# A Hymba-style decoder layer: six depthwise filters as three half-length ones, gate dots off VectorE, and a planner that knows the shared port

## The chip, the cores and the metric

The kernel runs on one core of one Trainium2 chip, in one launch. The metric is the device time of an execution in microseconds (us), the median of several runs. A profile of one execution is read beside it. Engines are named as in the profile: PE is TensorE (PEld its weight loads), DVE is VectorE, ACT is ScalarE, POOL is GpSimd, SP is SyncE, which issues the DMAs.

## The reference

x is 1024 tokens of 1024 channels in float32; there is one layer.

```python
mod = silu(c) @ mod_w + mod_b                       # shift, scale, gate: 1024 each
h = rmsnorm(x, norm_g) * (1 + scale) + shift
u = h @ w_in                                        # 5 x 1024 columns: cv, cg, cs, lx, ls
v = cv * sigmoid(cg)
v = causal_depthwise_conv(v, dw_w, dw_b)            # 31 taps along the tokens, per channel
v = silu(layernorm(v, cln_g, cln_b))
y_conv = (v @ pw2_w + pw2_b) * silu(cs)
xs = causal_depthwise_conv(lx, sc_w, sc_b)          # 4 taps
r, i = sigmoid(xs @ wr + br), sigmoid(xs @ wi + bi) # 8 heads of 128
a = exp(-8 * r * softplus(-lam))
h_t = a_t * h_{t-1} + sqrt(1 - a_t^2) * (i_t * xs_t)
y_lru = h * silu(ls)
x = x + (1 + gate) * (concat(y_conv, y_lru) @ w_out)
out = rmsnorm(x, final_g)
```

## The kernel before

Channels lie on the 128 partitions and the 1024 tokens along a row, so a tile is 128 x 1024 and each 1024-wide tensor is eight tiles. Each matmul is done as three, on numbers split into a high part and a rest: high by high, high weight by rest, rest of the weight by high (`uh`, `ul`, `yh`, `yl` for data, `whi`, `wlo` for weights; `xsh`, `xsl` for the input of the gates). ACT makes a high part, DVE or POOL the rest. A weight tile takes 48 matmuls of 512 columns.

The stages: four weight tiles (`FIRST`, the conv value and gate of channels 0 and 1) run on x before its norm is known, and are scaled by `rbc` (the norm's factor, spread over the partitions by small matmuls from sums of squares, `sq`) and shifted by `bias` afterwards. Then 36 weight tiles of `w_in` follow, numbered 4 to 39, and with them, for each of eight heads i, two gate matmuls (`gate`, L928) behind the tile that makes `xs` of that head, whose four-tap filter runs on DVE. Weight tiles 40 to 47 are the second half of `w_out`, on the recurrent half's result. In between come the conv tiles: six of eight are filtered on DVE (`conv_tile`, 30 SCALAR_TENSOR_TENSOR in place on `cacc`, the only accumulator in PSUM of its pool, after a first pass on ACT), tiles 2 and 5 (`POOLED`) by products on ACT and sums on POOL. `csum` adds the eight; the mean of the layer norm is a matmul on it. The last stage does the pointwise projection and the first half of `w_out` as products on quarters of the matrices, with fewer multiplications.

The conditioning's 24 rows of 1024 are dot products on DVE (`modw`): eight for scale and eight for shift at the start, eight for `gate1` later (`gate_mod`), which the last additions need.

No order is written out by hand. `Plan` gathers operations with an engine, an estimated cost, a priority (mostly the number of the weight tile; conv tiles have 1000 + 5 i, so they fill gaps), the tiles they read and write, and goes through time, giving each engine the ready operation of lowest priority. What comes out is a fixed order for each engine's queue; on the chip an engine waits at the head of its queue and does nothing behind it. One rule of the planner is for GpSimd and VectorE, whose operations on two SBUF operands it lets run only one at a time:

```python
if o.lock:
    end = max(t, locked) + cost
    locked = end
```

The constants that the change touches: `GM` is the number of the weight tile with the first gate dot, `SQP` the priority of the squares of x.

Of the kernel before, what the change touches and what calls it, by code (L numbers as in the profile page):

```python
# [66 lines left out]
class Buf:  # L67
    def __init__(self, pool, name, dtype, parts):
        self.pool, self.name, self.dtype, self.parts = pool, name, dtype, parts
        self.left, self.tile = 0, None  # L70

# [4 lines left out]
class Op:  # L76
    __slots__ = ("eng", "cost", "emit", "prio", "table", "bufs", "succ", "wait", "ready",
                 "seq", "reserve", "columns", "lock", "end")


class Plan:
# [23 lines left out]
    def op(self, eng, cost, emit, prio, r=(), w=(), table=None, after=(), reserve=0,  # L105
# [25 lines left out]
        for b in o.bufs:  # L131
            b.left += 1
        self.ops.append(o)
        return o

    def order(self):
# [9 lines left out]
        locked = 0.0  # L146
        left = len(self.ops)
        while left:
            while releases and releases[0][0] <= t:
                free[heapq.heappop(releases)[2]] += 1  # L150
            moved = False
            for e in engines:
                if until[e] > t + 1e-9:
                    continue
                best, key = None, None
                for o in pending[e]:
# [9 lines left out]
                    if any(free[p] < n for p, n in need.items()):  # L166
                        continue
# [15 lines left out]
                if o.lock:  # L183
                    end = max(t, locked) + cost
                    locked = end
                o.end = end
                until[e] = end
                out.append((t, o))
                for b in o.bufs:
# [3 lines left out]
                    b.left -= 1  # L193
                    if b.left == 0 and b.pool in free:
                        heapq.heappush(releases, (end, b.name, b.pool))
                for s in o.succ:
                    lat = 0.0 if e == "PE" and s.eng == "PE" else 0.11 if e == s.eng == "DVE" else self.LATENCY[e]
                    s.ready = max(s.ready, end + lat)
                    s.wait -= 1
                    if s.wait == 0:  # L200
                        pending[s.eng].append(s)
            if not moved:
                nxt = [u for u in until.values() if u > t + 1e-9]
# [17 lines left out]
def hymba_layer(ctx: ExitStack, tc: tile.TileContext, xT, c_row, vecs, mod_w, w_first, w_in,  # L221
# [205 lines left out]
    def acc_tile(name, parts=2):  # L427
        return S.buf("acc", name, F32, parts)
# [405 lines left out]

    v, c = {}, {}
    csum = big_buf("csum")

    def conv_tile(i):
# [388 lines left out]
```

## Time and profile before

| what | us |
|---|---|
| median of three runs (769.9 to 771.56) | 771.23 |
| the profiled execution | 771.67 |
| its span, first to last instruction | 769.1 |
| PE busy | 733.7 (95%) |
| PEld busy | 605.0 (79%) |
| DVE busy | 699.6 (91%) |
| ACT busy | 400.6 (52%) |
| POOL busy | 313.4 (41%) |

The mean granted TensorE clock is 0.985 of full speed. "Busy" adds up the time in which an engine has an instruction running. A wait row names the engine that waited, and whose work ended the wait. A group row names the source line (of a helper in most cases), engine and operation, output and inputs, shapes and count, then busy time, mean of one in ns, and idle time before them with who ended it. A timeline row has start, duration, engine, line and operation, and in brackets the idle time just before it.

### The profile page before, as it was taken

To read this page: it belongs to the slowest core of one execution; us is meant where nothing else is said; L and a number is where in the kernel's file an instruction comes from. 1 tells how busy PE (TensorE), PEld (TensorE's weight loads), DVE (VectorE), ACT (ScalarE), POOL (GpSimd) and SP (SyncE) were. 2 spreads that over 40 slices of the span, in tenths; PEclk is the share of its full clock that TensorE was granted. 3 is DMA by queue.
4 is the path that set the end of the run, shared out by engine and by line. 5 is a ranking of instruction groups with operands and counts; after the bars stand their busy time and mean duration, and the time that the engine had idled before them with its cause. 6 is when DMAs were issued, how large, how long until landed. Compare 5 with 4: busy or idle time off the path is not lost.

```text
span 769.1 us, 8497 instructions
## 1 busy us (share of the span) xinstructions
PE 733.7 (95%) x3288; PEld 605.0 (79%) x3288; DVE 699.6 (91%) x720; ACT 400.6 (52%) x432; POOL 313.4 (41%) x124
## 2 busy tenths in 40 slices
PE   3998999999999999999997999999999999999995
PEld 2887778888888788888885888887888888887885
DVE  7989999999999999999999979999699976998565
ACT  6720737987516479755525575514575223544220
POOL 0040123999996769999981226122120000000000
PEclk9999999999999999999998999999999999999997
DMA  9940221323321112112110012334333432325114
GB/s 339 392 153 1 84 82 35 110 82 110 117 82 56 35 55 83 34 55 83 50 60 28 28 55 82 137 137 143 131 110 110 164 110 71 121 83 178 41 55 165
DMA packets 24951, 77.81 MB, mean 101 GB/s; under 512 B 2768, under 2 KB 6096, under 8 KB 24912
## 3 DMA queue, kind: packets, MB, share of 16 engines
q1 hardware_dynamic: 24912, 77.28, 28.3%
q8 instruction: 26, 0.43, 0.2%
q14 instruction: 13, 0.11, 0.0%
HBM read 64.68 MB, written 12.58 MB: 100 GB/s over the span
## 4 chain that ended last, share of the span: by engine, by line
PE 66%; DVE 14%; POOL 14%; issue 2%; DMA 2%; ACT 1%; DVEq 0%; POOLq 0%; SPq 0%; ACTq 0%
PE ps L410 43%; POOL c L292 9%; PE papw L531 5%; PE pbpw L531 4%; POOL wlo L292 3%; PE paout L531 3%; PE out L577 3%; DVE ul L284 2%; DVE cacc L284 2%; PE gate L928 2%; PE pbout L531 2%; PE first L639 2%; DVE modw L284 2%; DMA fraw<-in_w_first_dram 1%; DVE xs L284 1%
## 5 line engine op out<-in xcount | busy, mean ns | idle before, releaser
L292 POOL TENSOR_TENSOR wlo<-raw,whi 128x1024 fp32r<-128x1024 f32 x44 | 122.7, 2788 | 235.1 <-ACT whi L265 235.1
L410 PE MATMUL ps<-uh,wlo 128*128 128x512 f32 x576 | 178.3, 391 | 3.3 <-POOL wlo L292 3.2
L410 PE MATMUL ps<-ul,whi 128*128 128x512 f32 x576 | 178.0, 390 | 1.4 <-DVE ul L284 1.4
L410 PE MATMUL ps<-uh,whi 128*128 128x512 f32 x576 | 178.0, 390 | 0.0
L292 POOL TENSOR_TENSOR c<-c,cq 128x1023 f32<-128x1023 f32 (+29 forms) x60 | 160.0, 2667 | 7.7 <-ACT cq L273 5.0
L284 DVE SCALAR_TENSOR_TENSOR cacc<-sig,V,cacc 128x994 f32<-128x994 f32 (+28 forms) x116 | 147.2, 1269 | 3.4 <-ACT cacc L273 0.6
L410 PEld LDWEIGHTS ps<-uh,wlo 128*128 128x128 f32 x576 | 108.1, 188 | 27.2 <-POOL wlo L292 5.0
L410 PEld LDWEIGHTS ps<-ul,whi 128*128 128x128 f32 x576 | 108.4, 188 | 24.4 <-DVE ul L284 1.8
L410 PEld LDWEIGHTS ps<-uh,whi 128*128 128x128 f32 x576 | 108.3, 188 | 22.7
L265 ACT CAST whi<-raw 128x1024 fp32r<-128x1024 f32 x48 | 50.2, 1046 | 53.9 <-issue 26.6
L284 DVE SCALAR_TENSOR_TENSOR cacc<-first_u,V,cacc 128x994 f32<-128x994 f32 (+28 forms) x58 | 73.5, 1268 | 1.2
L273 ACT ACTIVATE cq<-sig,V 128x1023 f32<-128x1023 f32 (+29 forms) x60 | 63.7, 1127 | 2.3 <-POOL c L292 2.3
L273 ACT ACT_TABLE_LOAD x46 | 59.0, 1283 | 1.5 <-PEq L1219 0.7
L284 DVE SCALAR_TENSOR_TENSOR modw<-modw,sc 128x1024 f32<-128x1024 f32 x24 | 41.5, 1740 | 1.6 <-DMA modw<-in_mod_w_dram 1.6
L265 ACT CAST xsh<-xs 128x1024 fp32r<-128x1024 f32 x8 | 8.4, 1048 | 61.9 <-DVE xs L284 61.9
L410 PE MATMUL ps<-yh,whi 128*128 128x512 f32 x128 | 40.0, 394 | 0.0
L410 PE MATMUL ps<-yl,whi 128*128 128x512 f32 x128 | 39.5, 390 | 0.0
L410 PE MATMUL ps<-yh,wlo 128*128 128x512 f32 x128 | 39.4, 389 | 0.0
L639 PE MATMUL first<-uh,fhi 128*128 128x512 f32 x64 | 26.8, 418 | 12.5 <-ACT uh L273 11.0
L284 DVE SCALAR_TENSOR_TENSOR xs<-ps,V,xs 128x1023 f32<-128x1023 f32 (+2 forms) x24 | 30.6, 1275 | 3.4 <-ACT xs L273 3.4
L410 PEld LDWEIGHTS ps<-yh,whi 128*128 128x128 f32 x128 | 23.9, 188 | 5.2 <-issue 0.5
L410 PEld LDWEIGHTS ps<-yh,wlo 128*128 128x128 f32 x128 | 24.0, 188 | 5.1
(292 smaller groups left out, 1331.0 us busy)
## 6 DMA issues: line engine op xcount, KB each, us to landing
raw<-in_w_in_dram SPq DMA_DIRECT2D x36, 512.0 KB, 3.4
modw<-in_mod_w_dram SPq DMA_DIRECT2D x24, 512.0 KB, 5.4
raw<-in_w_out_dram SPq DMA_DIRECT2D x12, 512.0 KB, 4.2
scsd<-scs SPq DMA_DIRECT2D x8, 512.0 KB, 3.0
acc<-in_xT_dram SPq DMA_DIRECT2D x8, 512.0 KB, 5.3
accd<-acc SPq DMA_DIRECT2D x8, 512.0 KB, 2.9
rawpw<-in_pw_dram SPq DMA_DIRECT2D x8, 512.0 KB, 3.4
scsr<-scsd SPq DMA_DIRECT2D x8, 512.0 KB, 4.5
```

The lines of the kernel that those rows point to most:

```text
L265: act.copy(out(), in_())
L273: act.activation(out=out(), in_=in_(), func=func, **kw)
L284: dve.scalar_tensor_tensor(out=out(), in0=in0(), scalar=scalar, in1=in1(), op0=op0, op1=op1, accum_out=accum)
L292: lambda: e.tensor_tensor(out=out(), in0=a(), in1=b(), op=op), prio, r, w,
L410: pe.matmul(ps()[:, a - off:b - off], k3(lhs)()[:, k, :], rhs[k]()[:, a:b], start=(k == 0 and lhs is wh and rhs is xh and (a - off) % H == 0),
L531: pe.matmul(half(*ps)(), half(*lhs)()[:, j * P:j * P + P], half(*rhs)(), start=start and j == 0 and z == 0, stop=j == KT // 2 - 1 and z == ...
L577: pe.matmul(ps()[:, a - off:e - off], k3(lhs)()[:, k, :], rhs()[:, i * H + a % H:i * H + a % H + e - a], start=k == KORD[0] and lhs is wh ...
L639: pe.matmul(ps()[:, a:b], fw_part(lhs, k, i * P, i * P + P)(), rhs()[:, a:b], start=k == 0 and lhs is wh and rhs is xh, stop=k == KT - 1 a ...
L928: pe.matmul(ps()[:, c0:c1], lhs()[:, j, :], rhs()[:, c0:c1], start=st == 0, stop=st == 2)
```

## The change

Six conv tiles (all but `POOLED`): with the tile's tokens apart into even ones `ev` and odd ones `od`, the 31-tap filter becomes three of half length: the even taps on `ev` (16 taps, `acc_e`), the odd taps on `od` (15), and the sums of neighbouring taps on `ev + od` (16 taps, in `acc_s`). The odd outputs are the third less the other two, the even outputs the first plus the second one token later. The first pass of each is on ACT, the others are SCALAR_TENSOR_TENSOR on DVE; `acc_s` is copied out by ACT and then holds the odd taps. `v` is written with even and odd tokens apart by the operation that makes it. The sums of taps (`wsum`) are made once.

The eight gate dots: the product on POOL, its sum and the addition of the bias on ACT, from weight tile 22 on rather than 12.

The planner: a POOL operation that finds the port taken by DVE starts when it comes free, and an operation on PSUM waits until the other engines' work on that PSUM tile is through. The squares of x get priority -90 rather than -60.

```diff
-GM = 12
+GM = 22
+TAPP = -15
-SQP, RSP, BIP, HHP, HCH, EVP = -60, -110, -50, -40, 0.1, -80
+SQP, RSP, BIP, HHP, HCH, EVP = -90, -110, -50, -40, 0.1, -80
...
+        def clear(o):
+            return max((e + self.LATENCY[g] for b, w in o.psum
+                        for d in ((b.read, b.written) if w else (b.written,))
+                        for g, e in d.items() if g != o.eng), default=0.0)
...
+                if e == "POOL" and waiting and held["DVE"] <= t + 1e-9:
+                    o, waiting, moved = waiting, None, True
+                    held["POOL"] = t + o.cost
+                    done(o, t + o.cost)
...
+                    if o.psum and clear(o) > t + 1e-9:
+                        later.append(clear(o))
+                        continue
...
-        acc = acc_tile(f"cacc{i}")
-        ACT(pr, acc, vi, AF.Identity, scale=w(0), bias=vec("dw_b", i), r=[vi, ("V", 1)], w=[acc])
-        for s in range(TAPS - 1, 0, -1):
-            if s == 1:
-                ACT(pr, part(ci, 0, 1), part(acc, 0, 1), "copy", 1, r=[acc], w=[ci])
-            to = ci if s == 1 else acc
-            STT(pr, part(to, s, T), part(vi, 0, T - s), w(s), part(acc, s, T), ALU.mult,
-                ALU.add, T - s, r=[vi, acc], w=[to])
+        acc, b2 = acc_tile(f"cacc{i}"), bias2[:, i:i + 1]
+        acc_e, acc_s, src_s = half(acc, 0), half(acc, 1), half(ci, 0)
+        ev, od = (lambda: vi()[:, :H]), (lambda: vi()[:, H:])
...
+        TT(pr, "DVE", src_s, ev, od, ALU.add, H, r=[vi], w=[(ci, 0)])
+        ACT(pr, acc_e, ev, AF.Identity, H, scale=w(0), bias=vec("dw_b", i), r=[vi, ("V", 1)],
+            w=[(acc, 0)])
+        ACT(pr, acc_s, src_s, AF.Identity, H, scale=ws(0), bias=b2,
+            r=[(ci, 0), ("V", 1), ("wsum", 0)], w=[(acc, 1)])
+        for r in range(1, 16):
+            STT(pr, cut(acc_e, r, H), cut(ev, 0, H - r), w(2 * r), cut(acc_e, r, H), ALU.mult,
+                ALU.add, H - r, r=[vi, (acc, 0)], w=[(acc, 0)])
+            STT(pr, cut(acc_s, r, H), cut(src_s, 0, H - r), ws(r), cut(acc_s, r, H), ALU.mult,
+                ALU.add, H - r, r=[(ci, 0), (acc, 1)], w=[(acc, 1)])
+        ACT(pr, every(1), acc_s, "copy", H, r=[(acc, 1)], w=[ci])
+        ACT(pr, acc_s, od, AF.Copy, H, scale=w(1), r=[vi], w=[(acc, 1)])
+        for r in range(1, 15):
+            STT(pr, cut(acc_s, r, H), cut(od, 0, H - r), w(2 * r + 1), cut(acc_s, r, H), ALU.mult,
+                ALU.add, H - r, r=[vi, (acc, 1)], w=[(acc, 1)])
+        ACT(pr, every(0), acc_e, "copy", H, r=[(acc, 0)], w=[ci])
+        TT(pr, "DVE", every(1), every(1), acc_e, ALU.subtract, H, r=[ci, (acc, 0)], w=[ci])
+        TT(pr, "DVE", every(1), every(1), acc_s, ALU.subtract, H, r=[ci, (acc, 1)], w=[ci])
+        TT(pr, "DVE", cut(every(0), 1, H), cut(every(0), 1, H), cut(acc_s, 0, H - 1), ALU.add,
+           H - 1, r=[ci, (acc, 1)], w=[ci])
...
-            TT(pr, "DVE", v[i], ps, v[i], ALU.mult, r=[ps, v[i]], w=[v[i]])
+                v[i] = big_buf(f"v{i}")
+                TT(pr, "DVE", apart(v[i], 0, T), by_two(ps, 0, T), by_two(sg, 0, T), ALU.mult,
+                   r=[ps, sg], w=[v[i]])
...
-        STT(n, m, m, 1.0, sc, ALU.mult, ALU.mult, accum=a, r=[m, sc], w=[m, ("macc", 16 + j)])
-        S.op("DVE", 0.08, lambda: dve.tensor_tensor(
-            out=gate1[:, j:j + 1], in0=a, in1=b1[:, KT + j:KT + j + 1], op=ALU.add), n,
-            [("macc", 16 + j), ("b1", 0)], [("gate1", j)])
+        dot("POOL", n, 2 * KT + j)
+        ACT(n, lambda: gate1[:, j:j + 1], lambda: a, AF.Identity, 1,
+            bias=b1[:, KT + j:KT + j + 1], r=[("macc", 2 * KT + j), ("b1", 0)], w=[("gate1", j)])
```

What comes of it in the queues, at three places. A name has the index of its tile behind it (`xs5` is head 5's xs, `cacc6` conv tile 6's accumulator, `ps31` weight tile 31), then a buffer number; `x2` at the end means two instructions in a row.

First DVE, where xs of head 5 is filtered for the gate matmul that waits for it. Before:

```order
L292 TENSOR_TENSOR sls4_2576<-sls4_2576,r4_2652 128x1024
L292 TENSOR_TENSOR sig7_2744<-ps30_2734,sig7_2744 128x1024
L284 SCALAR_TENSOR_TENSOR cacc6_2785<-sig6_2356,V_80,cacc6_2785 128x995
L292 TENSOR_TENSOR yl4_2829<-sls4_2576,yh4_2820 128x1024
L284 SCALAR_TENSOR_TENSOR cacc6_2785<-sig6_2356,V_80,cacc6_2785 128x996
L284 SCALAR_TENSOR_TENSOR cacc6_2785<-sig6_2356,V_80,cacc6_2785 128x997
L284 SCALAR_TENSOR_TENSOR cacc6_2785<-sig6_2356,V_80,cacc6_2785 128x998
L284 SCALAR_TENSOR_TENSOR cacc6_2785<-sig6_2356,V_80,cacc6_2785 128x999
L284 SCALAR_TENSOR_TENSOR cacc6_2785<-sig6_2356,V_80,cacc6_2785 128x1000
L284 SCALAR_TENSOR_TENSOR cacc6_2785<-sig6_2356,V_80,cacc6_2785 128x1001
L284 SCALAR_TENSOR_TENSOR cacc6_2785<-sig6_2356,V_80,cacc6_2785 128x1002
L284 SCALAR_TENSOR_TENSOR xs5_2881<-ps31_2803,V_80,xs5_2881 128x1023
```

Now:

```order
L312 SCALAR_TENSOR_TENSOR cacc6_2612<-v6_2511,V_80,cacc6_2612 128x501
L312 SCALAR_TENSOR_TENSOR xs5_3010<-ps31_2924,V_80,xs5_3010 128x1023
L312 SCALAR_TENSOR_TENSOR cacc6_2612<-v6_2511,V_80,cacc6_2612 128x500
L312 SCALAR_TENSOR_TENSOR xs5_3010<-ps31_2924,V_80,xs5_3010 128x1022
L312 SCALAR_TENSOR_TENSOR cacc6_2612<-v6_2511,V_80,cacc6_2612 128x499
L312 SCALAR_TENSOR_TENSOR xs5_3010<-ps31_2924,V_80,xs5_3010 128x1021
L320 TENSOR_TENSOR yl3_3057<-sls3_2244,yh3_3047 128x1024
L320 TENSOR_TENSOR xsl5_3074<-xs5_3010,xsh5_3059 128x1024
L312 SCALAR_TENSOR_TENSOR cacc6_2612<-v6_2511,V_80,cacc6_2612 128x498
L320 TENSOR_TENSOR c6_2529<-c6_2529,cacc6_2612 128x512
```

Conv tile 6 was at its first taps here and is now at the last of its third filter; between the taps of xs there are still conv taps, now of half length, and head 3's yl stands ahead of xsl.

Second, PE around the layer norm's mean. Before:

```order
L410 MATMUL ps41_3565<-yh7_3493,whi41_3512 128x512 x2
L410 MATMUL ps41_3565<-yl7_3504,whi41_3512 128x512 x2
L410 MATMUL ps41_3565<-yh7_3493,wlo41_3517 128x512 x2
L964 MATMUL mean_3632<-csum_1931,ones_d_89 128x512 x2
L410 MATMUL ps42_3641<-yh0_1143,whi42_3572 128x512 x2
```

Now:

```order
L438 MATMUL ps39_3583<-uh6_413,wlo39_3508 128x512 x2
L1043 MATMUL mean_3651<-csum_1773,ones_d_89 128x512 x2
L438 MATMUL ps39_3583<-uh7_441,whi39_3502 128x512 x2
L438 MATMUL ps39_3583<-ul7_458,whi39_3502 128x512 x2
L438 MATMUL ps39_3583<-uh7_441,wlo39_3508 128x512 x2
L438 MATMUL ps40_3662<-yh0_1124,whi40_3590 128x512 x2
```

The mean stood behind weight tile 41 and now stands six matmuls before the end of tile 39.

Third, DVE at the start, where the last `ul` of the first pass is made. Before:

```order
L292 TENSOR_TENSOR sq1_186<-sq1_186,sq5_313 128x1024
L284 SCALAR_TENSOR_TENSOR ul6_406<-x6_321,gs_93,uh6_397 128x512 x2
L284 SCALAR_TENSOR_TENSOR ul7_419<-x7_358,gs_93,uh7_408 128x1024
L284 SCALAR_TENSOR_TENSOR modw0_372,macc_96<-modw0_372,sc_121 128x1024
L284 SCALAR_TENSOR_TENSOR modw1_381,macc_96<-modw1_381,sc_121 128x1024
```

Now:

```order
L320 TENSOR_TENSOR sq1_188<-sq1_188,sq7_388 128x1024
L723 SCALAR_TENSOR_TENSOR gs_93<-macc_96,b1_97,V_80 128x1
L312 SCALAR_TENSOR_TENSOR modw15_338,macc_96<-modw15_338,sc_123 128x1024
L312 SCALAR_TENSOR_TENSOR ul6_426<-x6_323,gs_93,uh6_413 128x512 x2
L776 RECIPROCAL st_101<-st_101 128x8
L723 SCALAR_TENSOR_TENSOR gs_93<-macc_96,b1_97,V_80 128x1
L312 SCALAR_TENSOR_TENSOR modw0_372,macc_96<-modw0_372,sc_123 128x1024
L312 SCALAR_TENSOR_TENSOR modw1_383,macc_96<-modw1_383,sc_123 128x1024
L312 SCALAR_TENSOR_TENSOR ul7_458<-x7_358,gs_93,uh7_441 128x1024
```

The sums of squares (two more of them ahead of it than before), the reciprocal for `rbc` and two shift dots have moved ahead of `ul7`.

More of the change, by code (lines that the diff above doesn't have):

```diff
@@ L70, in __init__ @@
         self.left, self.tile = 0, None
+        self.read, self.written = {}, {}
     def __call__(self):
@@ L132, in op @@
             b.left += 1
+        o.psum = [(b, any(k[0] is b for k in w)) for b in o.bufs if b.pool in ("mm", "acc")]
         self.ops.append(o)
@@ L192, in order @@
                         free[b.pool] -= 1
[L193 to L201, printed above, removed]
+                if e == "POOL" and held["DVE"] > t + 1e-9:
+                    waiting, until[e] = o, float("inf")
+                    continue
+                if o.lock:
+                    if e == "DVE":
+                        end = max(t, held["POOL"]) + cost
+                    held[e] = end
+                done(o, end)
             if not moved:
-                nxt = [u for u in until.values() if u > t + 1e-9]
+                nxt = later + [u for u in until.values() if t + 1e-9 < u < float("inf")]
                 nxt += [o.ready for e in engines for o in pending[e] if o.ready > t + 1e-9]
@@ L996, in hymba_layer @@
             if s[1] < CG:
-                dst, sg = part(t, a, e), part(sig[j], a, e)
-                rd = tk + halves(sig[j], a, e)
-                STT(p + 3, dst, dst, bi, sg, ALU.add, ALU.mult, n, r=rd + [("bias", 0)], w=tk)
+                if a == 0:
+                    v[j] = big_buf(f"v{j}")
+                STT(p + 3, apart(v[j], a, e), by_two(t, a, e), bi, by_two(sig[j], a, e), ALU.add,
+                    ALU.mult, n, r=tk + halves(sig[j], a, e) + [("bias", 0)], w=[v[j]])
         if s[1] >= CG:
```

56 lines of the change are left out of this document (45 added, 11 removed).

## The prediction

> **What bounds the kernel now.** I read the totals first, then TensorE by stretches of 20 us, then who made TensorE wait, then the one place where it waited longest. The totals of the page:
>
> ```profile
> span 769.1 us, 8497 instructions
> PE 733.7 (95%) x3288; PEld 605.0 (79%) x3288; DVE 699.6 (91%) x720; ACT 400.6 (52%) x432; POOL 313.4 (41%) x124
> ```
>
> TensorE is idle for 769.1 - 733.7 = 35.4 us, and the change takes no matmul away. So the question is how much of 35.4 us, and of time at half clock, it can give back. The stretches in which TensorE is not full (columns: stretch; length, then busy us of PE, PEld, DVE, ACT, POOL with instructions; granted clock; DMA):
>
> ```profile
> 0.00:20.00 20.00, 7.66 (x25) 5.87 (x26) 15.10 (x47) 13.67 (x19) 0.70 (x6) 1.00 0.91 342
> 20.00:40.00 20.00, 20.00 (x90) 16.54 (x89) 20.00 (x34) 15.43 (x22) 0.57 (x1) 1.00 0.93 364
> 40.00:60.00 20.00, 19.21 (x97) 15.79 (x95) 17.77 (x27) 3.41 (x7) 7.30 (x4) 0.91 0.42 144
> 60.00:80.00 20.00, 18.54 (x84) 15.01 (x85) 19.04 (x39) 0.58 (x1) 0.00 (x0) 1.00 0.02 3
> 80.00:100.00 20.00, 17.73 (x83) 14.19 (x82) 19.37 (x25) 19.15 (x26) 5.47 (x2) 1.00 0.22 78
> 260.00:280.00 20.00, 17.68 (x79) 14.31 (x78) 19.74 (x13) 9.47 (x10) 11.07 (x4) 1.00 0.16 53
> 400.00:420.00 20.00, 14.52 (x51) 10.96 (x50) 19.72 (x17) 7.10 (x7) 3.50 (x2) 0.83 0.17 52
> ```
>
> A full stretch holds 90 matmuls, 0.222 us each. The first stretch (12.3 us idle, the first loads) and what comes behind 590 us keep their order of matmuls, so I leave both as they are. What is left: 40 to 100 us is idle for 0.79 + 1.46 + 2.27 = 4.5 us, 260 to 280 for 2.3 us, 400 to 420 for 5.5 us. A clock of 0.91 over 20 us, if it is halved or whole, means 3.6 us at half clock, 1.8 us of work lost; 0.83 means 6.8 us and 3.4 us lost. The waits by name (engine, line, waited for; us, times, longest):
>
> ```profile
> PE gate L928 <- ACT xsh L265: 5.4, 1, 5.4
> PE ps L410 <- POOL wlo L292: 3.2, 2, 2.3
> PE ps L410 <- DVE ul L284: 1.4, 1, 1.4
> PE first L639 <- DVE first_u L292: 0.8, 1, 0.8
> PE first L742 <- ACT rbc L265: 0.7, 1, 0.7
> PE first L639 <- ACT rbc L265: 0.7, 1, 0.7
> ```
>
> The longest one, head 5's gate matmul, named ACT's copy xsh. The timeline there tells who was really late:
>
> ```profile
> 395.13 1.20 ACT L273 ACTIVATE xs<-ps,V 128x1024 f32<-128x1024 f32 x1
> 396.39 9.04 DVE L284 SCALAR_TENSOR_TENSOR cacc<-sig,V,cacc 128x996 f32<-128x996 f32 x7
> 405.35 1.27 DVE L284 SCALAR_TENSOR_TENSOR xs<-ps,V,xs 128x1023 f32<-128x1023 f32 x1
> 406.54 1.26 DVE L284 SCALAR_TENSOR_TENSOR cacc<-sig,V,cacc 128x1003 f32<-128x1003 f32 x1
> 411.43 1.04 ACT L265 CAST xsh<-xs 128x1024 fp32r<-128x1024 f32 x1 [15.10 <-DVE xs L284]
> 412.53 1.22 PE L928 MATMUL gate<-xsh,ghi 128*128 128x512 f32 x2 [5.44 <-ACT xsh L265]
> ```
>
> xs is ready for its short filter at 396.33, but seven conv taps stand ahead of it on DVE, and it begins at 405.35: DVE is 9 us behind there. DVE is the second bound, full from 60 to 520 us beside a TensorE that is nearly full:
>
> ```profile
> 60.00:100.00 40.00, 36.27 (x165) 29.20 (x166) 38.41 (x63) 19.74 (x27) 5.47 (x2) 1.00 0.12 41
> 100.00:400.00 300.00, 297.50 (x1309) 245.01 (x1308) 296.49 (x213) 186.54 (x181) 253.55 (x95) 1.00 0.21 71
> 400.00:520.00 120.00, 114.52 (x492) 93.75 (x491) 113.12 (x88) 59.86 (x56) 33.81 (x13) 0.97 0.23 79
> ```
>
> DVE is busy for 448.0 of 460 us, TensorE idle for 11.7.
>
> **The change part by part.** First what it does to DVE.
>
> ```profile
> L284 DVE SCALAR_TENSOR_TENSOR cacc<-sig,V,cacc 128x994 f32<-128x994 f32 (+28 forms) x116 | 147.2, 1269 | 3.4 <-ACT cacc L273 0.6
> L284 DVE SCALAR_TENSOR_TENSOR fin<-paout,gate,fin 128x512 f32<-128x512 f32 x4 | 2.9, 746 | 0.1
> L292 DVE TENSOR_TENSOR yc<-yc,scsr 128x512 f32<-128x512 f32 x12 | 8.2, 687 | 0.1
> L284 DVE SCALAR_TENSOR_TENSOR x<-x,gs,rbc 128x512 f32<-128x512 f32 x16 | 13.6, 880 | 0.0
> ```
>
> *Conv tiles.* A tile costs 30 taps of 1.269 us now, 38.1 us. It becomes 15 + 15 + 14 = 44 taps of half the length and four half-length TENSOR_TENSOR. A half tap with one operand in PSUM is the 746 ns row. Such rows overlap their successor: taps of two chains begin 406.54 - 405.35 = 1.19 us apart though each lasts 1.27, while seven of one chain take 9.04 / 7 = 1.29 each. So a half tap takes 0.746 - 0.08 = 0.67 us in the two chains that alternate (30 of them, 20.1 us) and 0.77 alone (14, 10.8 us); with 4 x 0.687 the tile takes 33.6 us. That saves 4.5 us a tile, 27 us in six. Bounds: all at 0.67 save 5.9 a tile, 35 us; all at the 880 ns of the two-SBUF-operand row, the dearest half-length row near, cost 44 x 0.88 + 2.7 = 41.4 and lose 20 us. I take the first, since the taps keep PSUM as an operand and their 116 rows average as if nothing held them. Whether reading and writing every second token costs more no row shows; it concerns five rows a tile, and even doubled DVE loses 6 x 4 x 0.69 = 16 us: the same side of the bound.
>
> [...]
>
> *Gate dots.* All eight leave DVE (columns of the first row: DVE's busy time in the dots from 75 to 255 us, that is of these eight alone):
>
> ```profile
> 75.00:255.00 180.00, 19.58 (x16) 1.00 0.24 84
> L953 DVE TENSOR_TENSOR gate<-macc,b 128x1 f32<-128x1 f32 x8 | 10.6, 1321 | 0.0
> 262.01 3.31 POOL L292 TENSOR_TENSOR csum<-c,c 128x1024 f32<-128x1024 f32 x1 [4.32 <-DVE c L284]
> 265.28 4.32 POOL L292 TENSOR_TENSOR wlo<-raw,whi 128x1024 fp32r<-128x1024 f32 x1
> ```
>
> 19.6 + 10.6 = 30.2 us of DVE go. GpSimd gets eight products of at most 4.32 us, 35 us in all; from 100 to 400 us it has 46 to spare (253.55 busy), and from 400 to 520 it is busy for 33.81 of 120. Only the wlo halves on it are urgent. ScalarE gets eight sums and eight small adds, and in each conv tile three more passes of half length; by the 1.20 us of the xs pass that is 8 x 1.2 + 18 x 0.6, 20 us, at 52% busy: hidden, unless its queue waits (rivals). The gate weights' loads move with the dots, ten weight tiles later on SP's queue, where the DMA engines are 21 to 23% busy: nothing. So DVE's 448.0 us fall to 448 - 27 - 30 = 391.
>
> [...]
>
> *What must fit.* In the new order the mean matmul stands two weight tiles and six matmuls earlier, 102 matmuls:
>
> ```profile
> 522.52 21.80 PE ps L410 x96
> 519.19 1.23 DVE L292 TENSOR_TENSOR csum<-csum,c 128x1024 f32<-128x1024 f32 x1
> ```
>
> 96 take 21.8 us, so 102 take 23.2, and DVE must have csum ready that much sooner, and sooner again by whatever TensorE gains. With no idle time of TensorE left that is 460 - 23.2 - 11.7 = 425 us for 391 us of work: 34 us, some 6 us a tile, for waits in DVE's queue.
>
> *What TensorE gets back.* (a) 400 to 420.
>
> ```profile
> L940 DVE TENSOR_TENSOR_SCAN r<-a,xs 128x1024 f32<-128x1024 f32 x8 | 27.4, 3424 | 0.0
> L292 DVE TENSOR_TENSOR sls<-sls,r 128x1024 f32<-128x1024 f32 x8 | 16.7, 2083 | 0.1
> L292 DVE TENSOR_TENSOR xs<-xs,r 128x1024 f32<-128x1024 f32 x8 | 16.0, 1995 | 0.0
> ```
>
> In the new order DVE has, between head 4's gates and xs of head 5, head 4's scan (3.4), sls (2.1) and three products of 2.0 at most, eleven taps of 0.77, and v with two half sums (1.27 + 2 x 0.69): 22.6 us. TensorE has three weight tiles there, 32.7 us (the 96-matmul row), so DVE arrives early. From xs at 395.13 the chain is then 1.20, three steps of 1.19, two half taps of 0.67, and yl and xsl, of sls's kind, 2.1 each: 10.3 us, and TensorE has 54 matmuls, 12.2 us, before it needs it. The wait goes with its half clock: 5.5 + 3.4 = 8.9 us (0 to 8.9). (b) 260 to 280: wlo stood behind csum on GpSimd, which waited for DVE's second conv tile; 2.3 us (0 to 2.3). (c) 40 to 100.
>
> ```profile
> L736 PE MATMUL first<-ones,sq 128*128 128x1 f32 x32 | 3.8, 248 | 0.1
> L742 PE MATMUL first<-ident,st 128*128 128x128 f32 x16 | 2.3, 286 | 0.7 <-ACT rbc L265 0.7
> L292 DVE TENSOR_TENSOR sq<-sq,sq 128x1024 f32<-128x1024 f32 x6 | 7.3, 1218 | 0.0
> ```
>
> Squares and their sums come earlier; six matmuls now stand between the two parts of the spread and its copy (1.4 us of waits go), and first_u is drained earlier (0.8); of the 1.8 us of clock I take half: 3.1 us. Against it, two sums of squares and two shift dots (2 x 1.22 and 2 x 2.45 at most, from 19.58 / 8) now stand ahead of the last ul on DVE, 7.3 us, and so does a reciprocal that waits for TensorE's sums and holds up the last gs, those dots and that ul. What covers them is that the sums' and the spread's matmuls, 3.8 + 2.3 = 6.1 us, now stand ahead of the matmuls that read this ul; what is over, 1.2 us, is the other bound: -1.2 to 6.3.
>
> (d) New waits. The planner puts the gate matmuls of heads 5 and 6 and the mean where it thinks their operands ready, with nothing to spare; before, csum ended at 520.42 (519.19 + 1.23) and the matmuls behind the mean began at 522.52, with no room but the mean itself between. The trace cannot price this beforehand: 0, or the 8.9 us of (a) once more. I take two waits as long as the one for wlo, 2 x 2.3 = 4.6, nearer to that row than to (a) since DVE has room; a wait of that length left the clock whole at 260 to 280.
>
> Sum: 8.9 + 2.3 + 3.1 - 4.6 = 9.7 us. The profiled execution took 771.67 us (span 769.1 and 2.6 around it), 0.44 over the median 771.23; 771.67 - 9.7 = 762.0, and at the median's level 761.5.
>
> **The rivals.** *All waits go*: (d) is 0 and (c) 6.3, 771.2 - 17.5 = 753.7. For it: DVE's room. Against: three matmuls without slack.
>
> *The change does not lighten DVE*: half taps cost 0.88 us each, the conv part loses the 20 us that the dots give mostly back, DVE stays at 438 us and 425 are there. Then (a) comes back elsewhere and only (b) and part of (c) stay: 770, between 767 and 773. Against it: the 746 ns row.
>
> *The hand-over costs more than the taps save* (slower). There is one accumulator in PSUM, now in two halves. Behind the last tap of the sum filter ScalarE must copy it out and refill it before the third filter can begin, in its queue's turn, where it was held for 15.10 us above. Before, DVE waited for ScalarE's accumulator 0.6 us in all. Two hand-overs of 5 us each are 10 us a tile, 60 in six, 26 over the room: the mean waits for csum by that, with 1.7 us of half clock behind it, 771.2 - 14.3 + 26 + 1.7 = 785. It decides from (34 + 12.6) / 6 = 7.8 us a tile on. For it: tile 7 has nothing between its two filters. Against: in tiles 1, 3 and 4 two products of a head's chain stand between them, about 4 us, and in tile 6 the whole chain with its scan.
>
> **How the numbers follow.** Forecast 0.53 (757 to 768), all waits go 0.12, DVE not lightened 0.13, hand-over 0.22. About 0.2%, 1.5 us, is what a measurement can tell from no change. Faster: 0.53 + 0.12 + 0.06 = 0.71; same: 0.05 of the third case; slower 0.22 + 0.02 = 0.24. The range 754 to 774 leaves out half of the second case and most of the fourth, 0.2.
>
> [...]
>
> **What would show it.** Right: DVE near 640 us in all, half taps at 0.75, no gate wait over 2.5 us, the stretch that was 400 to 420 at full clock, and PE idle near 30 us. Wrong: DVE waiting for ScalarE's copies over 5 us a tile, TensorE waiting at the mean, or half taps near 0.88.

## The result and the profile after

| | before | changed |
|---|---|---|
| median of 20 runs, us | 770.89 | 770.90 |
| lowest to highest, us | 768.02 to 771.95 | 769.16 to 775.07 |
| profiled execution, us (span) | 771.67 (769.1) | 771.28 (769.4) |

The ratio is 1.0012, with a 95% interval of 0.9998 to 1.0026: no change, where 761.5 us were forecast. The totals of the changed kernel:

```profile
span 769.4 us, 8629 instructions
PE 733.5 (95%) x3288; PEld 606.0 (79%) x3288; DVE 665.6 (87%) x806; ACT 420.3 (55%) x473; POOL 323.1 (42%) x132
```

DVE has 34 us less to do and TensorE waits as long as before: 769.4 - 733.5 = 35.9 us for 35.4. So what was freed did not reach TensorE, or was lost again. The stretches (same columns as in the prediction) tell that it is the second:

```profile
80.00:100.00 20.00, 16.42 (x72) 12.84 (x71) 20.00 (x24) 17.25 (x23) 7.63 (x2) 0.95 0.30 100
260.00:280.00 20.00, 20.00 (x90) 16.57 (x89) 19.74 (x19) 11.05 (x14) 11.04 (x4) 1.00 0.26 96
280.00:300.00 20.00, 18.42 (x82) 14.91 (x81) 16.97 (x21) 18.33 (x22) 20.00 (x9) 1.00 0.18 63
300.00:320.00 20.00, 15.81 (x60) 12.54 (x59) 17.77 (x22) 16.18 (x20) 19.84 (x9) 0.83 0.28 105
400.00:420.00 20.00, 20.00 (x90) 16.39 (x89) 16.60 (x15) 13.14 (x13) 19.77 (x9) 1.00 0.24 76
460.00:480.00 20.00, 17.59 (x71) 14.12 (x70) 17.54 (x20) 10.39 (x11) 4.99 (x2) 0.92 0.19 66
```

400 to 420 and 260 to 280 are full now, at full clock. In their place 80 to 100, 280 to 320 and 460 to 480 have holes. Their waits, with the longest in the last column:

```profile
PE ps L438 <- ACT scs L301: 6.6, 2, 4.2
PE ps L438 <- DVE ul L312: 3.6, 2, 3.4
PE ps L438 <- POOL wlo L320: 1.6, 1, 1.6
PE gate L1008 <- ACT sls L301: 0.3, 1, 0.3
```

Because TensorE runs the weight tiles in the same order in both kernels, the start of one and the same matmul shows where time goes:

| matmul (weight tile, number in it) | before | changed | changed less before |
|---|---|---|---|
| 4, first | 68.43 | 65.20 | -3.23 |
| 6, 17th | 96.89 | 92.20 | -4.69 |
| 6, 33rd (behind the wait for ul) | 101.74 | 101.59 | -0.15 |
| 21, 17th (wlo, 260 to 280) | 272.51 | 269.98 | -2.53 |
| 23, 17th (a wlo of GpSimd) | 294.27 | 293.62 | -0.64 |
| 24, 17th (behind the wait for scs3) | 307.87 | 314.02 | +6.15 |
| 33, first | 405.56 | 411.04 | +5.47 |
| 33, 17th (behind head 5's gate matmul) | 420.78 | 417.49 | -3.29 |
| 38, 17th (behind the wait for scs5) | 480.62 | 482.15 | +1.53 |
| 47, 33rd | 587.72 | 589.49 | +1.77 |

The long wait comes about so (ScalarE's timeline, then TensorE's row; in brackets the idle time before it and what ended that):

```profile
297.37 1.03 ACT L301 ACTIVATE sls<-ps 128x1024 f32<-128x1024 f32 x1
303.53 1.06 ACT L301 ACTIVATE modw<-modw 128x1024 f32<-128x1024 f32 x1 [5.14 <-POOL modw L320]
306.88 1.01 ACT L301 ACTIVATE scs<-ps 128x1024 f32<-128x1024 f32 x1
307.95 1.22 PE L438 MATMUL ps<-uh,whi 128*128 128x512 f32 x2 [4.19 <-ACT scs L301]
```

ScalarE stands for 5.14 us at the sum of a gate dot whose product GpSimd has not made, and the drain that would give TensorE its PSUM buffer stands behind, though the last matmul into it ended at 301.04. The one at 474 looks alike, with the hand-over copy of conv tile 7 ahead of the drain of scs5. And the half taps, which were to give DVE room:

```profile
296.45 0.74 DVE L312 SCALAR_TENSOR_TENSOR cacc<-c,wsum,cacc 128x508 f32<-128x508 f32 x1
297.23 0.75 DVE L312 SCALAR_TENSOR_TENSOR cacc<-v,V,cacc 128x507 f32<-128x507 f32 x1
298.01 0.75 DVE L312 SCALAR_TENSOR_TENSOR cacc<-c,wsum,cacc 128x507 f32<-128x507 f32 x1
```

Taps of the two filters alternate, each lasts 0.75 us, and they begin 0.78 apart: nothing overlaps. All conv operations of the six tiles, from the start of each to the start of the next and without DVE's idle time, take 219.8 us, and the products that write their v 13.7 (2.2 of it a wait beside GpSimd); before it was 227.5 and 7.2. Six tiles save 1.2 us, not 27.

### The profile page after: what moved, and what is told of

It is laid out like the page before. It is cut to its first block, busy times and chain, and to the rows that moved or that the text cites. A ratio compares the mean times of both kernels' runs of the same rounds, so it can differ in the third digit from the quotient of the medians.

```text
span 769.4 us, 8629 instructions
## 1 busy us (share of the span) xinstructions
PE 733.5 (95%) x3288; PEld 606.0 (79%) x3288; DVE 665.6 (87%) x806; ACT 420.3 (55%) x473; POOL 323.1 (42%) x132
## 4 chain that ended last, share of the span: by engine, by line
PE 57%; DVE 29%; ACT 7%; POOL 3%; issue 2%; DMA 1%; SPq 0%; DVEq 0%; ACTq 0%; POOLq 0%
PE ps L438 32%; DVE cacc L312 11%; PE first L667 6%; PE papw L559 5%; PE pbpw L559 4%; PE out L605 3%; ACT cq L301 3%; PE paout L559 2%; DVE r L1020 2%; PE pbout L559 2%; DVE xs L312 1%; DVE xs L320 1%; DVE yl L320 1%; DVE sls L320 1%; POOL c L320 1%
## 5 line engine op out<-in xcount | busy, mean ns | idle before, releaser
L320 POOL TENSOR_TENSOR wlo<-raw,whi 128x1024 fp32r<-128x1024 f32 x44 | 115.1, 2615 | 234.5 <-ACT whi L293 234.5
L438 PE MATMUL ps<-uh,whi 128*128 128x512 f32 x576 | 180.5, 395 | 7.0 <-ACT scs L301 6.6
L312 DVE SCALAR_TENSOR_TENSOR cacc<-v,V,cacc 128x511 f32<-128x511 f32 (+14 forms) x174 | 129.6, 745 | 13.7 <-ACT c L293 6.3
L312 DVE SCALAR_TENSOR_TENSOR cacc<-c,wsum,cacc 128x511 f32<-128x511 f32 (+6 forms) x84 | 62.7, 746 | 2.3
L438 PEld LDWEIGHTS ps<-yl,whi 128*128 128x128 f32 x128 | 24.0, 188 | 5.0
L667 PE MATMUL first<-ul,fhi 128*128 128x512 f32 x64 | 26.3, 411 | 1.7 <-DVE ul L312 1.7
```

The source lines that it names most:

```text
L312: dve.scalar_tensor_tensor(out=out(), in0=in0(), scalar=scalar, in1=in1(), op0=op0, op1=op1, accum_out=accum)
L320: lambda: e.tensor_tensor(out=out(), in0=a(), in1=b(), op=op), prio, r, w,
L438: pe.matmul(ps()[:, a - off:b - off], k3(lhs)()[:, k, :], rhs[k]()[:, a:b], start=(k == 0 and lhs is wh and rhs is xh and (a - off) % H == 0),
L667: pe.matmul(ps()[:, a:b], fw_part(lhs, k, i * P, i * P + P)(), rhs()[:, a:b], start=k == 0 and lhs is wh and rhs is xh, stop=k == KT - 1 a ...
```

## The experiments

Each was timed in five rounds beside the kernel before. Ratios are to it.

| run | us | ratio (95%) |
|---|---|---|
| e1 two tiles | 765.2 | 0.9933 (0.9911 to 0.9955) |
| e2 drains first | 772.0 | 1.0013 (1.0000 to 1.0026) |
| e3 taps only | 784.9 | 1.0179 (1.0143 to 1.0216) |
| e4 dots only | 762.8 | 0.9891 (0.9856 to 0.9927) |
| e5 planner only | 781.2 | 1.0150 (1.0133 to 1.0167) |
| e6 no taps | 775.1 | 1.0065 (1.0043 to 1.0088) |
| e7 true costs | 758.3 | 0.9849 (0.9832 to 0.9866) |
| e8 taps only, two tiles | 772.6 | 1.0031 (1.0021 to 1.0040) |
| e9 tap costs | 765.0 | 0.9931 (0.9909 to 0.9953) |
| e10 scan cost | 764.1 | 0.9925 (0.9900 to 0.9950) |
| e11 two tiles, scan cost | 756.5 | 0.9814 (0.9795 to 0.9834) |
| e12 no taps, scan cost | 754.0 | 0.9785 (0.9766 to 0.9805) |
| e13 before, scan cost | 772.8 | 1.0040 (1.0027 to 1.0052) |
| e14 planner, scan cost | 776.0 | 1.0087 (1.0072 to 1.0101) |
| e15 dots, scan cost | 756.1 | 0.9823 (0.9809 to 0.9836) |
| e16 squares late | 763.6 | 0.9926 (0.9913 to 0.9938) |

**The shared PSUM tile (e1).** In the built program each half tap waits for the one issued just ahead, of the other filter. The edit gives each filter's accumulator a tile of its own:

```diff
-                    b.tile = pool.tile(shape, b.dtype, tag=tag, name=b.name)
+                    if b.pool == "acc":
+                        b.tile = Pair([pool.tile([P, H], b.dtype, tag=f"acc{i}", name=f"{b.name}_{i}")
+                                       for i in (0, 1)])
...
```

> The changed kernel, with the accumulator of a conv tile as two PSUM tiles of one bank each, one for the even and one for the sum filter, in place of two halves of one tile (for that, the products with mean and 1/std behind it are made in two halves, 16 more DVE operations behind 500 us). Theory A (the two filters serialise each other: a half tap starts only when the tap of the other filter, issued just ahead of it, has ended, because both write one PSUM tile; DVE is then about 20 us late over six tiles, and this lateness goes on to ScalarE and GpSimd and makes TensorE wait for both scs drains): alternating taps start 0.67 us apart where it was 0.785, DVE has 180 x 0.11 = 20 us more room before the mean, both waits for scs and the half clock behind them (6.8 and 4.2 us) shrink to under 1 us each: 760 us. Theory B (the waits come from what stands in ScalarE's queue ahead of the drains, whatever DVE does): the taps come closer, but only the drain behind the hand-over copy of tile 7, which waits for a DVE tap itself, gets better, and the one behind the gate dot's sum, which waits for GpSimd, stays: 767 us. If the halves' distance is DVE's own and not the shared tile's: 0.785 stays, 771 us.

The same taps in e1's timeline:

```profile
291.85 0.74 DVE L327 SCALAR_TENSOR_TENSOR cacc<-c,wsum,cacc 128x508 f32<-128x508 f32 x1
292.50 0.74 DVE L327 SCALAR_TENSOR_TENSOR cacc<-v,V,cacc 128x507 f32<-128x507 f32 x1
293.15 0.74 DVE L327 SCALAR_TENSOR_TENSOR cacc<-c,wsum,cacc 128x507 f32<-128x507 f32 x1
```

0.65 us apart for 0.78 in one tile, as theory A said: the distance is that of the shared tile, not DVE's own. The conv operations fall to 200.7 us, 33.5 a tile. The time falls by 5.7 us, half of the 11 that A gave and more than the 4 of B. The waits for scs shrink (3.3 us in all), and the mean waits 1.6 us for csum: half of A's account holds.

**Drains ahead (e2).** ScalarE's queue, the only thing that differs:

```diff
 ACTIVATE sls3<-ps22
+CAST whi25<-raw25
+ACTIVATE scs3<-ps23
 ACTIVATE modw19,macc<-modw19
 ACTIVATE gate1<-macc,b1
 ACTIVATE cq5_11<-sig5,V
-CAST whi25<-raw25
-ACTIVATE scs3<-ps23
...
 ACTIVATE sls7<-ps36
+ACTIVATE scs5<-ps37
 COPY c7<-cacc7
 ACTIVATE cacc7<-v7,V
 COPY c7<-cacc7
-ACTIVATE scs5<-ps37
```

> The changed kernel with two swaps in ScalarE's queue and nothing else moved on any engine: the drain of scs3 (the one TensorE waited 4.2 us for) stands ahead of the sum of a gate dot that waits for GpSimd, and the drain of scs5 (2.4 us) stands ahead of the two hand-over copies of conv tile 7 that wait for a DVE tap. Theory B (in-order ScalarE: the operations that the change added hold up PSUM drains): both waits and the half clock behind them go, 6.8 + 4.2 = 11 us: 760 us. Theory A (the engines behind are late as a whole): TensorE waits for the next late operand or drain instead (ul's wait is elsewhere; the sigmoid drains of the gates and xs of the next head are late too), 2 to 4 us come back: 767 to 769 us.

Nothing is won. Both waits for scs are gone from its list, and others stand there:

```profile
PE mean L1064 <- DVE csum L341: 4.6, 1, 4.6
PE ps L459 <- POOL wlo L341: 4.2, 3, 2.3
PE gate L1029 <- DVE xsl L341: 1.7, 1, 1.7
```

Theory B falls: the place in ScalarE's queue only chose where TensorE waited. The engines behind it were late as a whole.

**The parts alone (e3 to e6).** e3 has the conv code of the change with the old planner and DVE's dots, e4 the dots alone, e5 the planner alone (squares at the old place), e6 is the changed kernel with the old conv code. The lines that make them:

```diff
 e4, against before
-GM = 12
+GM = 22
-        STT(n, m, m, 1.0, sc, ALU.mult, ALU.mult, accum=a, r=[m, sc], w=[m, ("macc", 16 + j)])
+        dot("POOL", n, 2 * KT + j)
...
 e5, against before
-                if o.lock:
-                    end = max(t, locked) + cost
-                    locked = end
+                if e == "POOL" and held["DVE"] > t + 1e-9:
+                    waiting, until[e] = o, float("inf")
+                    continue
...
 e6, against the change (e3 the other way round, against before)
-        for r in range(1, 16):
-            STT(pr, cut(acc_e, r, H), cut(ev, 0, H - r), w(2 * r), cut(acc_e, r, H), ALU.mult,
...
+        for s in range(TAPS - 1, 0, -1):
...
+            STT(pr, part(to, s, T), part(vi, 0, T - s), w(s), part(acc, s, T), ALU.mult,
```

> The kernel before with the three half-length filters alone (old planner, gate dots on DVE at tiles 12 to 19). The prediction's step (27 us less DVE work in six tiles, 4.5 a tile) would let the gate-5 wait of 8.9 us go: 762 us. By the taps as the changed kernel shows them (30 alternating ones 0.785 us apart, 14 alone 0.773, four sums of 0.68 to 1.4 and 0.8 more for the product that sorts even and odd tokens) a tile takes 38.5 us of DVE where it took 38.1: nothing is freed, and the planner, which books 0.66 us a tap, puts the urgent matmuls too early: 772 to 778 us, with DVE's busy time within 15 us of the 700 before.

> The kernel before with the gate dots alone moved to GpSimd and ScalarE, at tiles 22 to 29 (old planner, old conv taps). If DVE's lateness made the gate-5 wait, 30 us less on DVE let it go: about 762 us, DVE's busy time near 670. If what GpSimd and ScalarE take on holds up their urgent work (halves of weights, drains), the gain is eaten there: 768 to 774 us, with TensorE waiting for wlo or for a ScalarE drain near the dots' tiles (280 to 350 us).

> The kernel before with the new planner alone (old conv taps, dots on DVE at tiles 12 to 19). If the three parts of the change simply add up (dots alone 762.8, taps alone 784.9, all of it 771), planner and earlier squares are worth -5.4: 765 to 766 us. If the planner only repairs what the taps spoil (it books ScalarE's and DVE's use of PSUM banks), there is nothing to repair here: 769 to 772 us, with the gate-5 wait of some 5 us still there.

> The changed kernel with the old conv taps (full-length, one chain of 30): dots, planner and earlier squares stay. If the taps are what ate the gain and the rest adds up: 762.8 - 5.4 = 757 us, TensorE idle under 25 us. If planner and squares only pay together with the taps: 761 to 764 us, as with the dots alone.

The dots alone give 8.4 us, and the taps alone cost 13.8, though DVE's conv work is not longer with them. e3, e5 and e6 came out 7, 9 and 11 us above every range given ahead, so none of the readings offered there accounts for their size. Waits of e3, in its list:

```profile
PE ps L411 <- POOL wlo L293: 9.1, 2, 6.0
PE mean L1017 <- DVE csum L293: 5.4, 1, 5.4
PE gate L981 <- ACT xsh L266: 4.1, 2, 2.1
```

The planner alone costs 11.5 us (769.7 before, in its job), and the sum of the parts is no guide: e6 is slower than e4, with the same dots. Three waits at places where the plan leaves nothing to spare point to the plan's own numbers.

**What the plan believes (e7, e9, e10).** It books 0.66 us for a half tap and no dependence between the two filters: with 0.78 measured, 0.12 too little 30 times a tile. And it books 2.2 us for the scan, outside the lock that it keeps for other DVE operations with two SBUF operands. DVE's scan in the changed kernel, at 459.96 with GpSimd idle until 461.62, at 491.24 with GpSimd at work:

```profile
459.96 2.27 DVE L1020 TENSOR_TENSOR_SCAN r<-a,xs 128x1024 f32<-128x1024 f32 x1
490.33 2.67 POOL L320 TENSOR_TENSOR wlo<-raw,whi 128x1024 fp32r<-128x1024 f32 x1 [10.12 <-ACT whi L293]
491.24 3.90 DVE L1020 TENSOR_TENSOR_SCAN r<-a,xs 128x1024 f32<-128x1024 f32 x1
```

The second scan ends 2.14 us behind the end of GpSimd's operation (490.33 + 2.67 = 493.00): it waited, then took its usual time. Five more scans that begin while GpSimd works end 2.14 or 2.15 us behind its operation, and the two that begin with GpSimd idle last 2.27 us each. An operation inside the lock looks alike: of the eight products sls, six begin while GpSimd works and end 1.07 or 1.08 us behind it, and the two others last 1.21. e7 has both edits, e9 the first, e10 the second:

```diff
-                ALU.add, H - r, r=[vi, (acc, 0)], w=[(acc, 0)])
+                ALU.add, H - r, r=[vi, acc], w=[acc])
-                ALU.add, H - r, r=[(ci, 0), (acc, 1)], w=[(acc, 1)])
+                ALU.add, H - r, r=[(ci, 0), acc], w=[acc])
...
-            pr, [a, xs], [r])
+            pr, [a, xs], [r], lock=True)
```

> The changed kernel with a planner that knows two things it does not know now: that the taps of the even and the sum filter follow each other as if they depended on each other (it books 0.11 us more for each), and that the scan, which takes 3.4 us on DVE where it books 2.2, waits for GpSimd's lock as other DVE operations with two SBUF operands do. The work is the same, only the order differs. If the false costs are why urgent matmuls and drains are put too early: the waits for scs (6.8 + 4.2 us) shrink, 763 to 766 us. If DVE simply has 20 us too much to do for any order: TensorE waits somewhere else for as long, 769 to 772 us.

> The changed kernel with the first of the two corrections alone: the planner books the taps of the even and sum filter as a chain (0.11 us more each, some 20 us over the six tiles); the scan stays at 2.2 us without the lock. If the taps' false cost made the waits (theory A2): 758 to 761 us, as with both. If the scan's did (theory S: eight scans of 3.4 us that are booked at 2.2, each at a place where the next gate matmul waits for DVE): 767 to 771 us.

> The changed kernel with the second correction alone: the scan waits for GpSimd's lock in the plan; the taps stay at 0.66 us with no dependence on each other. Theory A2 (taps): 767 to 771 us. Theory S (scan): 758 to 762 us. If each makes its own wait, both this and the run before lie between, near 764.

758.3 us, 12.6 less than the changed kernel, with not one instruction more or less of work: only the order differs. Each correction alone gives half (-5.9 and -6.9). The waits of e7, behind the one at the start:

```profile
PE ps L438 <- DVE ul L312: 3.6, 2, 3.4
PE paout L559 <- DVE l34out L320: 1.7, 1, 1.7
```

Both waits for scs and the one for wlo are gone, and from 100 to 400 us DVE is as busy as in the changed kernel (276.38 for 277.31 us):

```profile
100.00:400.00 300.00, 299.65 (x1320) 247.74 (x1319) 276.38 (x294) 205.23 (x219) 250.39 (x99) 1.00 0.20 69
```

So DVE had the room; the plan put it in the wrong places. Another order alone might have been luck, but the scan's lock was put into five more kernels (the runs that follow): four became 5 to 21 us faster, and only the kernel before did not (772.8 for 769.9).

**What the taps are worth (e8, e11, e12).** e8 is e3 with e1's two tiles, e11 is e1 with the scan's lock in the plan, e12 is e6 with it: three kernels of the edits above.

> The taps-only kernel (784.9 us) with the accumulator as two PSUM tiles, so that alternating taps start 0.65 us apart in place of 0.78; old planner, dots on DVE. If the shared tile is the whole cost of the taps: 771 us or under, since DVE then has 15 to 20 us less to do than in the kernel before. If the hand-over (ScalarE copies the sum out and fills the accumulator again, DVE waits for it, 9 us in all in the taps-only run) and the sorted product cost too: 775 to 780 us, with DVE waiting for ScalarE's cacc as long as before.

> The kernel with two PSUM tiles for the accumulator (765.2 us; its taps cost what the planner books), with the scan's lock in the plan as well, so that both costs are true and DVE has 20 us less to do than in the run with true costs (758.3). If only the plan's truth counts: 758 us, the same. If DVE's time still counts when the plan is true: 754 to 756 us.

> The changed kernel with the old full-length taps (775.1 us) and the scan's lock in the plan: dots, new planner and squares stay, and all costs are near the trace's. If the half-length filters earn nothing once the plan is true (38.5 us of DVE a tile against 38.1): 757 to 760 us, as the run with true costs. If they do earn (their parts are shorter and let urgent DVE work in between): 763 to 768 us.

Two tiles take 10.9 of the 13.8 us that the taps cost under the old planner (e8 is 2.9 us slower than the kernel before beside it). With a true plan the old, full-length taps are the fastest of all (754.0), by the medians 2.6 us ahead of the half taps in two tiles, which leave DVE 12 us less to do; the runs of the two just overlap (753.8 to 755.7 and 755.3 to 757.4). What TensorE waits for in e12, behind the start:

```profile
PE ps L437 <- DVE ul L311: 2.3, 3, 1.3
PE paout L558 <- DVE l34out L319: 1.7, 1, 1.7
```

Neither has to do with the conv tiles, so their taps can give no more.

**The planner and the squares (e13 to e16).** e13, e14 and e15 are the kernel before, e5 and e4 with the lock line of e7; e16 is e12 with

```diff
-SQP, RSP, BIP, HHP, HCH, EVP = -90, -110, -50, -40, 0.1, -80
+SQP, RSP, BIP, HHP, HCH, EVP = -60, -110, -50, -40, 0.1, -80
```

> The kernel before with one edit: its old planner lets the scan wait for GpSimd's lock. If the scan's false cost put head 5's gate matmul 9 us too early in the kernel before: that wait goes, 760 to 764 us. If the old planner's other errors (the lock as one clock for both engines, no PSUM waits) count as much: 768 to 773 us.

> The kernel before with the new planner and the scan's lock in it (dots on DVE at tiles 12 to 19, full-length taps, squares at the old place). The new planner alone gave 781.2. If the scan's cost is what it lacked: 763 to 767 us, 14 to 18 less, as the dots' kernel gained (775.1 to 754.0 = 21). If the loss sits at the start (TensorE waited 3.0 us for sq and 1.6 for shift near 60 us, with 13.7 us at half clock, 6.8 lost): about 775, and those rows stay.

> The dots alone (762.8) under the old planner with the scan's lock. If a true scan is all that the plan needs: 754 to 757 us, as the new planner with it (754.0). If the new planner's rules give something of their own: 759 to 763 us.

> The fastest kernel so far (754.0: dots, new planner, true scan, old taps) with the squares at their old place in the plan (priority -60 in place of -90). Term (c) of the prediction gave the earlier squares 3.1 us: by it this takes 757 us. If the planner alone lost its time to late squares (sq waited for 3.0 us and half clock behind it): 759 to 765 us. If the squares' place is worth nothing: 754 us.

A true scan alone gives the kernel before nothing. TensorE in e13 is nearly full up to 520 us, and waits behind it (stretches, then waits):

```profile
100.00:400.00 300.00, 299.91 (x1324) 248.00 (x1323) 296.04 (x218) 187.02 (x182) 253.99 (x95) 1.00 0.21 72
520.00:600.00 80.00, 70.03 (x300) 56.39 (x300) 68.59 (x73) 43.16 (x50) 9.61 (x4) 0.92 0.25 93
```

```profile
PE papw L531 <- DVE wlopw L292: 5.8, 1, 5.8
PE papw L531 <- DVE l34pw L292: 4.0, 1, 4.0
```

DVE is busy for 296 of 300 us in the first stretch: a true plan spares the gate matmuls (tile 33's 17th matmul starts 12.0 us sooner than before), but the last csum ends 3.7 us later, at 524.12, and what hangs on it takes the gain back. Room on DVE had to come first, from the dots. With the dots gone and the scan true the old planner reaches 756.1, the new one 754.0. The new planner's own loss sits at the start for the larger part: weight tile 4 begins 10.5 us later than in the kernel before in e5, 9.1 in e14 and 9.7 in e16, and 5 to 6 us of it are left at tile 9. Waits of e16, and its stretch from 60 to 80:

```profile
PE first L763 <- DVE sq L319: 3.4, 1, 3.4
PE first L666 <- DVE first_u L319: 1.4, 1, 1.4
```

```profile
60.00:80.00 20.00, 17.19 (x74) 14.86 (x74) 17.35 (x36) 5.08 (x7) 0.00 (x0) 0.68 0.18 53
```

So the earlier squares are worth 763.6 - 754.0 = 9.6 us (10.9 with each against the kernel before beside it), but this is shown under the new planner only, whose loss they mend.

## Why the prediction was wrong

*The bound and the dots: right.* The 30 us of dots left DVE (e4: DVE busy for 665.9 of 699.6), and e4 came out at 762.8. That this is near the 761.5 forecast of the whole is chance: e4 has neither the taps nor the squares.

*Conv tiles: the step "a half tap takes 0.746 - 0.08 = 0.67 us in the two chains that alternate" failed.* I took the overlap from two chains in two tiles (xs and cacc), while the two filters share one. It is 0.78. With that, and with the sorted product, 4.5 us a tile became 0.2. In two tiles the step holds (33.5 us a tile for 33.6). A half tap's length was right (0.75).

*(a) 8.9 us: 8.8 measured. (b) 2.3: 2.5 by the row of tile 21.* *(c) 3.1: nothing.* 4.7 us were won up to tile 6, and 4.5 lost there: the wait of 3.4 us for ul, and 3.2 us at half clock behind it (granted clock 0.50 from 98 to 101). Ahead of these ul on DVE stand the four products that write v of the first two conv tiles, sorted into even and odd tokens now. Before and changed, from DVE's timelines:

```profile
87.76 2.73 DVE L284 SCALAR_TENSOR_TENSOR first_u<-first_u,bias,first_u 128x512 f32<-128x512 f32 x4
```

```profile
85.29 3.32 DVE L312 SCALAR_TENSOR_TENSOR v<-first_u,bias,first_u 128x512 f32<-128x512 f32 x1
89.09 2.15 DVE L312 SCALAR_TENSOR_TENSOR v<-first_u,bias,first_u 128x512 f32<-128x512 f32 x2
```

2.15 / 2 = 1.08 us each for 2.73 / 4 = 0.68, and the first of them stood beside a wlo on GpSimd from 82.78 to 87.65. I had left the sorting at "no row shows". In e12, which has the old conv code and sorts nothing, the waits for ul are 2.3 us in all, no half clock follows them (granted clock 1.00 in every stretch from 40 to 560 us), and tile 15 begins at 195.25 for 198.27 in the kernel before: 3.0 us are kept there, the size of (c).

*(d) 4.6 us for three matmuls without slack: the wrong places.* Head 5's gate matmul, head 6's (0.3 us) and the mean hardly wait. 12.9 us come elsewhere: a wlo (1.9 by the table), scs3 (6.8) and scs5 (4.2). I looked for missing slack at the three matmuls that had moved; but the planner leaves none at any drain, so an error in its costs comes out wherever the late engine is needed next. e2 shows that these places are interchangeable, e7 that the error was in the plan's costs. I had both: 0.66 and 2.2 could be read in the code, and the scan's 3424 ns stood in a row that I quoted.

*The sum.* (a) 8.8, (b) 2.5, (c) 0.2 and (d) -12.9 make -1.4 where I had 9.7, and the table has 1.5 lost at tile 38. (d) failed above all: I priced new waits by DVE's room, and they came from the plan's false costs although room was there.

*"34 us of room": about right in size, and not what decided.* DVE up to the end of the last csum, at 499.13, and behind it up to 520 us, with the two largest groups of the second stretch:

```profile
60.00:499.13 439.13, 426.70 (x1854) 349.95 (x1852) 408.71 (x446) 282.66 (x300) 297.93 (x115) 0.98 0.20 68
499.13:520.00 20.87, 20.82 (x88) 16.58 (x89) 19.72 (x16) 12.13 (x12) 4.83 (x2) 1.00 0.34 126
L320 DVE TENSOR_TENSOR c<-c,mean 128x1024 f32<-128x1024 f32 x8 | 9.4, 1213 | 0.9 <-PE mean L1043 0.9
L320 DVE TENSOR_TENSOR lnss<-lnss,lnsq 128x1024 f32<-128x1024 f32 x6 | 8.9, 1490 | 0.2
```

Up to csum DVE is busy for 408.7 of 439.1 us, where I had worked out 391 of 425. That is 18 us more work: some 26 that the conv tiles did not save, less work that now lies outside the stretch, as 4.1 us of first_u's drains ahead of 60. The layer norm's work, which was behind 520 us before, follows at once. 30 us of room were there for 34, and did not help: e7, with 407.0 us of work up to its csum at 498.35, is 13 us faster. What GpSimd took over did not come back as waiting either: the seven operations of a head's chain on two SBUF operands (sls, yl, xsl, the scan, one product on r and two on xs) take 118.9 us in all for 119.0 before.

*The rivals.* "The change does not lighten DVE", 770 us, has the number, but not the cause: the conv part is indeed hardly lighter, but half taps never cost 0.88, DVE did not stay at 438, and with the same DVE time e7 takes 758. "All waits go", 753.7 us, is what e12 reaches, without the taps. The hand-over was not dear for DVE, in the changed kernel's list:

```profile
DVE cacc L312 <- ACT c L293: 6.3, 2, 4.3
DVE cacc L312 <- ACT cacc L301: 2.6, 1, 2.6
```

8.9 us in all are 1.5 a tile for the 7.8 from which it would decide; tile 7's copies did stand ahead of the drain of scs5, but e2 won nothing by moving it.

*The signs.* Half taps at 0.75, no gate wait over 2.5 us and a full clock from 400 to 420 came as named ahead, and none of the three signs of being wrong. Only DVE's 665.6 us for 640 and TensorE's idle 35.9 for 30 told of the miss: the signs looked where waits had been, not where they could go.

What is not settled: with the scan's cost false, the dots take 762.8 us under the old planner and 775.1 under the new one. That the old planner's cruder lock booked more time, and so hid the scan's error, would fit; no run tries it.

## What to carry to other kernels

Where a list scheduler sets the order, hold its cost of every operation against the trace, start to start and beside busy neighbours, before changing the work: here two false costs were worth 12.6 us, and a change that took 34 us off DVE gave nothing until they were mended. Look whether two chains that are to overlap share a tile: the half taps began 0.78 us apart in one tile and 0.65 in two (e1). And when swapping one waiting pair only moves the wait (e2), look for what is late as a whole.

## What the hardware showed beyond that

Two half taps in separate tiles (e1) begin 0.65 us apart and last 0.74; in one tile (the changed kernel), each waiting for the other, they begin 0.78 apart and last 0.75. The changed kernel's scan takes 2.27 us with GpSimd idle and 3.90 behind the GpSimd operation at 490.33. Sorting cost time where each element goes to the other half than its neighbour, and none was seen where every second one is read and written in place (groups of the changed kernel):

```profile
L320 DVE TENSOR_TENSOR v<-ps,sig 128x1024 f32<-128x1024 f32 x4 | 8.2, 2044 | 0.0
L320 DVE TENSOR_TENSOR c<-c,cacc 128x512 f32<-128x512 f32 (+1 forms) x18 | 11.9, 684 | 0.4
```

2.04 us for 1024 elements sorted, and 1.21 for the product `sig<-ps,sig` of the kernel before, which sorts nothing; 0.68 for 512 in place, and 0.69 for the product `yc<-yc,scsr` on 512 in a row.

One and the same wait for ul (3.4 us) had different prices. The stretch behind the one from 80 to 100 shown above (clock 0.95), then both of e9:

```profile
100.00:120.00 20.00, 19.64 (x84) 15.88 (x84) 19.48 (x27) 8.00 (x8) 4.81 (x2) 0.97 0.11 41
```

```profile
80.00:100.00 20.00, 16.57 (x65) 12.76 (x65) 20.00 (x23) 16.23 (x21) 7.62 (x2) 0.88 0.28 97
100.00:120.00 20.00, 19.65 (x82) 15.79 (x81) 17.77 (x25) 7.97 (x8) 4.78 (x2) 0.95 0.08 26
```

(0.05 + 0.03) x 20 / 0.5 = 3.2 us at half clock in the first, (0.12 + 0.05) x 20 / 0.5 = 6.8 in the second. Half clock is what the trace shows: in stretches of 1 us the granted clock of the changed kernel is 0.50 from 98 to 101 and 1.00 around that, but for the two stretches where it changes (0.93 and 0.86); in the kernel before it is 0.50 from 412 to 418, behind head 5's gate wait. Why e9 had it for longer no run shows. One kernel's own runs differ in the granted clock too. Of e4's, three took 758.5 to 760.4 us at a mean granted clock of 0.995 or 0.996 and three 765.1 to 765.5 at 0.987 or 0.988. 0.008 of 760 us is 6 us of clock, the distance between them, so the dots alone are worth 6 to 13 us by the clock that a run was granted; the profile, of one of the first three, has a granted clock of 1.00 in every stretch from 40 to 560 us.
